# Stream encoder: the sample's transposes and its last key chunk on 128 rows instead of 64

## The chip, the cores and the metric

The kernel runs on one core of one Trainium2 chip. The metric is device time in microseconds (us) of one execution.

## The reference

One inference step of a streaming encoder with four layers, A, B, C, A. Each layer computes x <- x + W_out(mixer(RMSNorm(x)) * silu(gate)) in fp32, and one input projection gives the mixer's inputs and the gate. There are two streams: a prompt of 512 frames without history, and a sample of 64 frames that follows a cache of past keys and values. All widths are for d_model 1024.

```
A: 8 heads of 128; 64-frame chunks attend a band of 9 chunks; bias by clipped distance; RMSNorm on q and k
B: 16 query heads, 4 key heads of 64; window 128 + own chunk; ALiBi, sinks; RMSNorm on q and k
C: latent attention, 16 heads of 64 + 32 rotary; latent of 256; causal by chunk; RMSNorm on q and k
sample: k = concat(cache, own 64 keys): 256 + 64 keys in A and C, 128 + 64 in B
        p = softmax(q k^T * scale + bias);  o = p v
```

Outputs are y for both streams and the new cache rows.

## The kernel before

The 576 frames (TOK) are worked on in five token tiles (TT): four of 128 frames for the prompt and one of 64 (DEC) for the sample. Frames lie on partitions (rows of TensorE's array) wherever a norm is taken, and on columns wherever a projection reads them, so each result is transposed on TensorE by `tr` (L166) into a PSUM tile `t` and copied from there. `tr(out, in_, rows, perm)` loads the data as the stationary operand with as many rows as the tile has frames, and streams that many columns of a permutation: the identity, or a reversed order (flip for 128 frames, flip2 for two halves of 64). For the sample tile rows is 64. These transposes occur in `norm` (two sets of four in each of four layers), in the q and k units of the A layers (four each, in eight head-pair units), in B's key unit (four) and four query units (two each), and in C's query latent (four), key latent (two and one of 32 columns), four query units (four of 96 columns) and eight key and value units (one each).

The large projections are split into a high and a low part in a reduced-width fp32 format (fp32r) and take three products (L151 to L153, L211 to L213); for the sample tile two products do, because its high and low parts lie side by side and fill 128 frames (L156, L157). Scores and value products of softmax are plain fp32 and appear as two TensorE instructions each.

The softmax of the sample has 128 rows: in A and C two heads of 64 queries. Its weights `ex` have 320 columns in A and C: two chunks of 128 cached keys and a last one of 64 own keys; in B there are 128 and 64 for each of two head pairs. They are transposed chunk by chunk; the last chunk is transposed from 64 columns, and its product with the values (`vt[:64, 4]`, L403, L633, L884) uses 64 rows:

```
for c, cn in ((0, 128), (1, 128), (2, 64)):
    tr(pt[:cn, c, :], ex[:, 128 * c : 128 * c + cn], 128, flip2)
S.activation(pts[:, 0:2, :], pt[:, 0:2, :], AF.Copy)
S.activation(pts[:64, 2, :], pt[:64, 2, :], AF.Copy)
PE.matmul(po[:, e, :], vt[:64, 4, 128 * e : 128 * e + 128], pts[:64, 2, r], start=False, stop=True)
```

Buffers rotate: `qs` (results ahead of a transpose) has four, `ex` four, `pts` and the PSUM tile `t` two, the A layers' values `v` two. Within a layer `mix` interleaves the attention of one head pair with the projections of the next pair and the gate of the one before. The order on each engine is then set by the framework's scheduler, which places instructions by simulated times; each engine works through its queue in that order. SyncE issues the DMAs. Layer pools reuse memory as soon as the tile that lay there is done. GpSimd takes the powers for the norms (L104), half of the weight splits (L109), rotary products (L696 to L700), the gate's product (L219) and a few memsets (L353, L821, L822). Layer B's constants, the sinks among them (`sks`, negated at L453 by VectorE), are loaded early.

Of the kernel before, what the change touches and what calls it, by code (L numbers as in the profile page):

```python
# [21 lines left out]
DEC = 64  # L22
# [18 lines left out]
def encoder_step(ctx: ExitStack, tc: tile.TileContext, I, O):  # L41
# [42 lines left out]

    x = []
# [79 lines left out]
    def tr(out, in_, rows, perm=None):  # L165
        PE.transpose(out, in_, (perm or ident)[:rows, :rows])  # L166
# [5 lines left out]
    def norm(t, g, xT):  # L172
        t0, tn = TT[t]
        ss = sb(1, "nss", pool=tiny)[:tn]
        junk = sb(D, "sq", 2, dt=BF16)[:tn]
        S.activation(junk, x[t][:tn], AF.Square, accum_out=ss)
        r = rstd(ss, tn, 1, 1.0 / D)
        for hf in range(2):
            xs = sb(512, "qs", QSB)[:tn]
            cs = slice(hf * 512, hf * 512 + 512)  # L180
            V.scalar_tensor_tensor(out=xs, in0=x[t][:tn, cs], scalar=r, in1=g[:tn, cs], op0=ALU.mult, op1=ALU.mult)
            pt = v3(ps_t(), 128)
            for j in range(4):
                tr(pt[:, j, :tn], xs[:, j * 128 : j * 128 + 128], tn)
            k0 = hf * 4
            l0 = lo_at(t0, TOK)
            hl_evac(xT[:, k0 : k0 + 4, t0 : t0 + tn], xT[:, k0 : k0 + 4, l0 : l0 + tn], pt[:, :, :tn])
            if tn == DEC:
                V.tensor_copy(xT[:, k0 : k0 + 4, 2 * TOK : WT], xT[:, k0 : k0 + 4, TOK : TOK + DEC].bitcast(F32))
# [69 lines left out]
    def layer_a(li, xT, first=None):  # L259
        w = I["a_w_in"][li]  # L260
        with tc.tile_pool(name=f"la{li}", bufs=1, reuse_waits="tile") as lp:
# [7 lines left out]
            def v_units(pr, pieces=None):  # L269
                st = [pieces] if pieces else []  # L270

                def unit(ts, tn):
                    if not st:
                        st.append(load_packed(w, 2048 + 256 * pr, 256))
                    if pr not in vs:
                        vs[pr] = v3(sb(5 * 256, "v", 2, pool=lp), 256)
                    vt = vs[pr]
                    p = ps_mm()
                    for i, t in enumerate(ts):
                        r_ = mm_tok(xT, TOK, 128 * t, tn, st[0], 256, p, 256 * i)  # L280
                    n = len(ts)
                    p = (p if n == 2 else r_)[:, : 256 * n]
                    S.activation(vt[:tn, ts[0] : ts[0] + n, :], v3(p, 256), AF.Copy)
                    for t in ts:
                        ld(O["av"][li, 128 * t : 128 * t + tn, 256 * pr : 256 * pr + 256], vt[:tn, t, :])

                return [lambda ts=ts, tn=tn: unit(ts, tn) for ts, tn in (((0, 1), 128), ((2, 3), 128), ((4,), 64))]

            def qk_units(pr):
                st = []  # L290

                def unit(t, t0, tn):
# [11 lines left out]
                    qs = sb(512, "qs", QSB)[:tn]  # L304
                    V.tensor_tensor(out=v3(qs, 128), in0=v3(p, 128), in1=bc(r.unsqueeze(2), tn, 4, 128), op=ALU.mult)
                    pt = v3(ps_t(), 128)
                    for j in range(4):
                        perm = ident if j > 1 else flip if tn == 128 else flip2
                        tr(pt[:, j, :tn], qs[:, j * 128 : j * 128 + 128], tn, perm)
# [23 lines left out]
            def attn_units(pr):  # L333
# [3 lines left out]
                def soft(s, bias, n):  # L337
                    nm = sb(1, "nm", pool=tiny)
                    tot = sb(1, "tot", pool=tiny)
                    ex = sb(512, "ex", 4)[:, :n]  # L340
                    V.tensor_tensor_reduce(out=ex, in0=s, in1=bias, scale=-1.0, scalar=1e38,
                                           op0=ALU.add, op1=ALU.min, accum_out=nm)
                    S.activation(ex, ex, AF.Exp, bias=nm, scale=-1.0, accum_out=tot)
                    softmax_tail(ex, tot, 128)
                    return ex

                def head(e, t):
# [18 lines left out]
                    for c in range(t + 1):  # L366
                        tr(pt[:, 128 * c : 128 * c + 128], ex[:, 128 * c : 128 * c + 128], 128, flip)
# [8 lines left out]
                def sample():  # L376
# [14 lines left out]
                    ex = soft(s, bs, 320)  # L391
                    pt = v3(ps_t(), 128)
                    for c, cn in ((0, 128), (1, 128), (2, 64)):
                        tr(pt[:cn, c, :], ex[:, 128 * c : 128 * c + cn], 128, flip2)
                    pts = v3(sb(512, "pts", 2), 128)
                    S.activation(pts[:, 0:2, :], pt[:, 0:2, :], AF.Copy)
                    S.activation(pts[:64, 2, :], pt[:64, 2, :], AF.Copy)
                    po = v3(ps_o()[:, :128], 64)
                    for e in range(2):
                        r = slice(64 * e, 64 * e + 64)  # L400
                        for c in range(2):
                            PE.matmul(po[:, e, :], vc[:, c, 128 * e : 128 * e + 128], pts[:, c, r], start=(c == 0), stop=False)
                        PE.matmul(po[:, e, :], vt[:64, 4, 128 * e : 128 * e + 128], pts[:64, 2, r], start=False, stop=True)  # L403
# [31 lines left out]
    def layer_b(xT):  # L435
        w = I["b_w_in"][0]
        with tc.tile_pool(name="lb", bufs=1, reuse_waits="tile") as lp:
# [23 lines left out]
            vt = v3(sb(5 * 256, "v", pool=lp), 256)  # L461
            vc = sb(256, "vc", pool=lp)
# [12 lines left out]
            for t, (t0, tn) in enumerate(TT):  # L475
# [7 lines left out]
                qs = sb(512, "qs", QSB)[:tn]  # L483
                for d in range(2):
                    V.tensor_tensor(out=v4(qs, 2, 64)[:, :, d, :], in0=v3(p[:, :256], 64), in1=bc(r.unsqueeze(2), tn, 4, 64), op=ALU.mult)
                pt = v3(ps_t(), 128)
                for j in range(4):
                    tr(pt[:, j, :tn], qs[:, j * 128 : j * 128 + 128], tn)
# [14 lines left out]
            def q_units(g):  # L503
                w_ = []

                def unit(t, t0, tn):
# [10 lines left out]
                    qs = sb(512, "qs", QSB)[:tn, :256]  # L517
                    V.tensor_tensor(out=v3(qs, 64), in0=v3(p, 64), in1=bc(r.unsqueeze(2), tn, 4, 64), op=ALU.mult)
                    pt = v3(ps_t()[:, :256], 128)
                    for j in range(2):  # L520
                        tr(pt[:, j, :tn], qs[:, j * 128 : j * 128 + 128], tn)
# [19 lines left out]
            def attn_units(g):  # L541
                st = {}

                def head(t):
# [36 lines left out]
                    for c in range(nk // 128):  # L581
                        pt = v4(ps_t(), 2, 128)
                        for e in range(2):
                            for j in range(2):
                                tr(pt[:, e, j, :], exs[e][:, j, 128 * c : 128 * c + 128], 128)
                        pts = v4(sb(512, "pts", 2), 2, 128)
                        if c == 0:
                            S.activation(pts, pt, AF.Copy)
                        else:
                            V.tensor_copy(pts, pt)  # L590
                        ptl.append(pts)
# [8 lines left out]
                def sample():  # L600
# [6 lines left out]
                    ex = v3(sb(512, "ex", 4)[:, :384], 192)  # L607
# [13 lines left out]
                    for j in range(2):  # L621
                        tr(pt[:, 0, j, :], ex[:, j, 0:128], 128)
                        tr(pt[:64, 1, j, :], ex[:, j, 128:192], 128)
                    pts = v4(sb(512, "pts", 2), 2, 128)
                    for c, rows in ((0, 128), (1, 64)):
                        S.activation(pts[:rows, c], pt[:rows, c], AF.Copy)
# [4 lines left out]
                    for e in range(2):  # L631
                        r = slice(64 * e, 64 * e + 64)
                        PE.matmul(po[r], vt[:64, 4, 64 * g : 64 * g + 64], pts[:64, 1, :, r], start=False, stop=True)  # L633
# [7 lines left out]

            run(q_units(0))
# [11 lines left out]
    def layer_c(xT):  # L654
        w = I["c_w_in"][0]
        with tc.tile_pool(name="lc", bufs=1, reuse_waits="tile") as lp:
# [50 lines left out]
            vslot = [v3(sb(7 * 128, f"v{j}", pool=lp), 128) for j in range(2)]  # L707

            pieces = load_chunk(w, [(0, 512)])
            for t, (t0, tn) in enumerate(TT):  # L710
# [5 lines left out]
                c = sb(512, "qs", QSB)[:tn]  # L716
                V.scalar_tensor_tensor(out=c, in0=p, scalar=r, in1=qag[:tn], op0=ALU.mult, op1=ALU.mult)
                pt = v3(ps_t(), 128)
                for j in range(4):
                    tr(pt[:, j, :tn], c[:, j * 128 : j * 128 + 128], tn)  # L720
# [4 lines left out]
            for t, (t0, tn) in enumerate(TT):  # L725
# [6 lines left out]
                c = sb(512, "qs", QSB)[:tn, :256]  # L732
# [4 lines left out]
                kr = sb(32, "kr", 2)[:tn]  # L737
# [4 lines left out]
                for j in range(2):  # L742
                    tr(pt[:, j, :tn], c[:, j * 128 : j * 128 + 128], tn)
                tr(pt[:32, 2, :tn], kr, tn)
# [14 lines left out]
            def q_units(g):  # L759
                st = {}  # L760

                def unit(t, t0, tn):
# [5 lines left out]
                    raw = sb(512, "qs", QSB)[:tn, :384]  # L768
# [12 lines left out]
                    for j in range(4):  # L781
                        tr(pt[:96, j, :tn], qs[:, j, :], tn)
# [6 lines left out]
            def kv_units(pr):  # L789
                kT, vt = kslot[pr % 2], vslot[pr % 2]  # L790

                def unit(ts, tn):
# [9 lines left out]
                    raw = sb(512, "qs", QSB)[:tn, : 128 * n]  # L802
# [9 lines left out]
                    pt = ps_t()[:, : n * tn]  # L812
                    for i in range(n):
                        tr(pt[:, 128 * i : 128 * i + tn], qs[:, 128 * i : 128 * i + 128], tn)
# [9 lines left out]
            def soft(s, n, mask):  # L824
                nm = sb(1, "nm", pool=tiny)
                ex = sb(512, "ex", 4)[:, :n]
# [13 lines left out]
            def attn_units(blk):  # L840
# [4 lines left out]
                def head(t, e):  # L845
# [9 lines left out]
                    for c in range(t + 1):  # L855
                        tr(pt[:, 128 * c : 128 * c + 128], ex[:, 128 * c : 128 * c + 128], 128)
# [11 lines left out]
                def sample():  # L868
# [4 lines left out]
                    ex = soft(s, 320, False)  # L873
                    pt = v3(ps_t(), 128)
                    for c, cn in ((0, 128), (1, 128), (2, 64)):
                        tr(pt[:cn, c, :], ex[:, 128 * c : 128 * c + cn], 128)
                    pts = v3(sb(512, "pts", 2), 128)
                    S.activation(pts[:, 0:2, :], pt[:, 0:2, :], AF.Copy)
                    S.activation(pts[:64, 2, :], pt[:64, 2, :], AF.Copy)
                    po = ps_o()[:, :64]  # L880
                    for c, cn in ((0, 128), (1, 128), (2, 64)):
                        for e in range(2):
                            r = slice(64 * e, 64 * e + 64)
                            PE.matmul(po[r], vt[:cn, 4 + c, r], pts[:cn, c, r], start=(c == 0), stop=(c == 2))  # L884
# [176 lines left out]
```

## Time and profile before

| | |
|---|---|
| median of three runs | 1302.87 us (1301.19 to 1304.98) |
| span of the profiled execution, first to last instruction | 1303.0 us |
| time of the profiled execution beside its span | not recorded apart from the span, which lies between the runs |
| TensorE busy | 1268.8 us (97%), 8119 matmuls or transposes and as many weight loads |
| VectorE, ScalarE, GpSimd busy | 718.3, 651.7, 376.2 us |
| mean granted clock of TensorE | 0.994 of 2.4 GHz |

The busy time of an engine is the time in which it had an instruction in work; matmuls overlap, so TensorE's busy share tells that it had work, not how fast the work went. In the profile's tables PE is TensorE's matmuls and transposes, PEld its weight loads, DVE VectorE, ACT ScalarE, POOL GpSimd; L166 is line 166. A form such as 64*128 64x64 is weights of 64 rows by 128 columns, and 64 rows by 64 columns streamed.

### The profile page before, as it was taken

The page shows a single profiled execution, that of the slowest core. Times are in us where ns is not written, and L with a number is a line of the kernel's source. Part 1 is how long each engine was busy: PE and PEld are TensorE (multiplying, and loading weights), DVE is VectorE, ACT ScalarE, POOL GpSimd, SP SyncE. Part 2 cuts the span into 40 slices and gives each one's busy share as a digit, 9 for nine tenths or more (in the row PEclk, how much of TensorE's full clock was granted, in tenths as well). Part 3 has the DMA queues.
Part 4 walks back from the last instruction along what each step waited for, and adds up shares of the span by engine and source line. Part 5 has one row for each costly group of instructions (what it writes and reads, how often), then busy time and mean ns, then how long its engine had stood idle before and what let it go on. Part 6 is the DMA issues. An engine that isn't in the chain of part 4 may idle for free.

```text
span 1303.0 us, 22559 instructions
## 1 busy us (share of the span) xinstructions
PE 1268.8 (97%) x8119; PEld 1099.4 (84%) x8119; DVE 718.3 (55%) x1983; ACT 651.7 (50%) x1665; POOL 376.2 (29%) x475
## 2 busy tenths in 40 slices
PE   4999999999999999999999999999999999999998
PEld 3889898998889888878898888877788898989986
DVE  3365444452668878626576766676164555444432
ACT  4245353552446766634356767686243454435431
POOL 3231212115025442140275453540401212121150
PEclk9899999999999999999999999999999999999999
DMA  5424141433446312144231101111244251414322
GB/s 160 129 91 137 58 134 51 153 100 95 151 123 215 88 56 80 56 143 147 61 109 45 46 25 50 34 36 49 88 160 128 92 155 54 142 50 134 126 82 73
DMA packets 101727, 127.21 MB, mean 98 GB/s; under 512 B 13296, under 2 KB 79760, under 8 KB 101552
## 3 DMA queue, kind: packets, MB, share of 16 engines
q1 hardware_dynamic: 101616, 125.77, 31.3%
q8 instruction: 64, 1.05, 0.3%
q14 instruction: 47, 0.39, 0.1%
HBM read 105.81 MB, written 24.26 MB: 100 GB/s over the span
## 4 chain that ended last, share of the span: by engine, by line
PE 93%; DMA 3%; DVE 1%; POOL 1%; ACT 1%; issue 1%; SPq 0%; DVEq 0%; ACTq 0%; POOLq 0%
PE mm L151 15%; PE mm L153 15%; PE mm L152 15%; PE t L166 9%; PE mm L211 5%; PE mm L212 5%; PE mm L213 5%; PE mm L156 4%; PE mm L157 4%; PE s L852 3%; PE o L371 3%; PE o L863 2%; PE s L363 2%; PE o L594 1%; DMA sks<-in_b_sinks 1%; DMA x<-in_x 1%
## 5 line engine op out<-in xcount | busy, mean ns | idle before, releaser
L104 POOL TENSOR_TENSOR nv<-nv,mhalf 128x4 f32<-128x4 f32 (+7 forms) x147 | 150.3, 1023 | 489.3 <-DVE nv L103 459.1
L151 PE MATMUL mm<-wh,T 128*128 128x256 f32 (+2 forms) x736 | 246.7, 339 | 3.2 <-ACT T L169 3.2
L153 PE MATMUL mm<-wh,T 128*128 128x256 f32 (+2 forms) x736 | 247.1, 338 | 0.0
L152 PE MATMUL mm<-wl,T 128*128 128x256 f32 (+2 forms) x736 | 244.7, 336 | 0.0
L108 ACT ACTIVATE wh<-ws 128x512 fp32r<-128x512 f32 (+2 forms) x288 | 169.6, 616 | 125.7 <-PE mm L156 74.5
L109 DVE TENSOR_TENSOR wl<-ws,wh 128x512 fp32r<-128x512 f32 (+2 forms) x252 | 170.0, 696 | 47.0 <-ACT wh L108 41.9
L211 PE MATMUL mm<-T,wh 128*128 128x288 f32 x512 | 154.8, 302 | 0.3 <-ACT sq L771 0.3
L213 PE MATMUL mm<-T,wl 128*128 128x288 f32 x512 | 154.1, 301 | 0.0
L151 PEld LDWEIGHTS mm<-wh,T 128*128 128x128 f32 x736 | 141.3, 192 | 15.2 <-ACT T L169 3.8
L212 PE MATMUL mm<-T,wh 128*128 128x288 f32 x512 | 152.8, 298 | 0.0
L153 PEld LDWEIGHTS mm<-wh,T 128*128 128x128 f32 x736 | 141.7, 193 | 12.9 <-issue 0.4
L152 PEld LDWEIGHTS mm<-wl,T 128*128 128x128 f32 x736 | 141.0, 192 | 11.9
L219 POOL TENSOR_TENSOR o<-o,sq 128x288 f32<-128x288 f32 x52 | 44.3, 852 | 227.2 <-DVE sq L217 139.9
L151 PE MATMUL mm<-wh,oT 128*128 128x512 f32 x256 | 99.2, 396 | 2.5 <-ACT oT L238 1.9
L153 PE MATMUL mm<-wh,oT 128*128 128x512 f32 x256 | 99.7, 397 | 1.2 <-POOL oT L241 1.2
L152 PE MATMUL mm<-wl,oT 128*128 128x512 f32 x256 | 100.2, 395 | 0.0
L211 PEld LDWEIGHTS mm<-T,wh 128*128 128x128 f32 x512 | 96.2, 188 | 4.7 <-issue 3.4
L166 PE MATMUL t<-ident,qs 128*128 128x128 f32 (+3 forms) x466 | 78.7, 277 | 20.1 <-DVE T L170 9.1
L212 PEld LDWEIGHTS mm<-T,wh 128*128 128x128 f32 x512 | 96.2, 188 | 1.8 <-issue 1.4
L213 PEld LDWEIGHTS mm<-T,wl 128*128 128x128 f32 x512 | 96.2, 188 | 1.4 <-issue 1.2
L166 PEld LDWEIGHTS t<-ident,qs 128*128 128x128 f32 (+3 forms) x466 | 54.4, 142 | 37.5 <-issue 10.6
L250 DVE TENSOR_TENSOR x<-mm,x 128x512 f32<-128x512 f32 x32 | 21.6, 690 | 112.5 <-PE mm L153 112.4
(233 smaller groups left out, 2666.9 us busy)
## 6 DMA issues: line engine op xcount, KB each, us to landing
ws<-in_a_w_in SPq DMA_DIRECT2D x64, 256.0 KB, 2.9
ws<-in_a_w_in SPq DMA_DIRECT2D x128, 128.0 KB, 2.4
ws<-in_b_w_in SPq DMA_DIRECT2D x40, 256.0 KB, 3.0
ws<-in_a_w_out SPq DMA_DIRECT2D x32, 256.0 KB, 3.2
xd<-x SPq DMA_DIRECT2D x12, 512.0 KB, 2.6
x<-xd SPq DMA_DIRECT2D x12, 512.0 KB, 5.9
ws<-in_c_w_in SPq DMA_DIRECT2D x24, 256.0 KB, 3.3
out_akT<-kf SPq DMA_DIRECT2D x8, 576.0 KB, 3.9
```

The source lines that it names most:

```text
L104: G.tensor_tensor(out=r, in0=r, in1=bc(mhalf[:tn], tn, n), op=ALU.pow)
L108: S.activation(h, src, AF.Copy)
L109: (eng or G).tensor_tensor(out=l, in0=src, in1=h.bitcast(F32), op=ALU.subtract)
L151: PE.matmul(out, xh, h[:, ws], start=(i == 0), stop=False)
L152: PE.matmul(out, xh, l[:, ws], start=False, stop=False)
L153: PE.matmul(out, xl, h[:, ws], start=False, stop=(i == last))
L156: PE.matmul(out, xs, h[:, ws], start=(i == 0), stop=False)
L157: PE.matmul(out, xs, l[:, ws], start=False, stop=(i == last))
L166: PE.transpose(out, in_, (perm or ident)[:rows, :rows])
L211: PE.matmul(p, wh, xT[:, k, cs], start=(k == 0), stop=False)
L212: PE.matmul(p, wh, xT[:, k, ls], start=False, stop=False)
L213: PE.matmul(p, wl, xT[:, k, cs], start=False, stop=(k == KD - 1))
```

## The change

Every transpose uses all 128 rows. The sample's results ahead of a transpose go into one of two standing tiles (`half`), whose lower 64 rows are set to zero once; `tr` no longer takes a row count. The sample's softmax weights go into one standing tile (`exz`) with zeros behind the last key, so that the last chunk is 128 wide; the values' fifth chunk gets zeros in its lower 64 rows by a memset per value tile, and the last product uses 128 rows. The two copies of the transposed weights become one. The framework's DMA scratch is set to 1024 bytes, which makes room. All that is added to the sums is zero.

```diff
+    half = [sb(512, f"half{i}", pool=const) for i in range(2)]
+    exz = sb(512, "exz", pool=const)
+    for z in half:
+        G.memset(z[DEC:], 0.0)
+    G.memset(exz, 0.0)
+    turn = [0]
+
+    def rows_of(tn):
+        if tn == 128:
+            return sb(512, "qs", QSB)
+        turn[0] ^= 1
+        return half[turn[0]]
...
-    def tr(out, in_, rows, perm=None):
-        PE.transpose(out, in_, (perm or ident)[:rows, :rows])
+    def tr(out, in_, perm=None):
+        PE.transpose(out, in_, perm or ident)
...
-            xs = sb(512, "qs", QSB)[:tn]
+            xs = rows_of(tn)
...
-                tr(pt[:, j, :tn], xs[:, j * 128 : j * 128 + 128], tn)
+                tr(pt[:, j, :], xs[:, j * 128 : j * 128 + 128])
...
                         vs[pr] = v3(sb(5 * 256, "v", 2, pool=lp), 256)
+                        G.memset(vs[pr][DEC:, 4, :], 0.0)
...
-                    ex = soft(s, bs, 320)
+                    soft(s, bs, 320, exz[:, :320])
                     pt = v3(ps_t(), 128)
-                    for c, cn in ((0, 128), (1, 128), (2, 64)):
-                        tr(pt[:cn, c, :], ex[:, 128 * c : 128 * c + cn], 128, flip2)
+                    for c in range(3):
+                        tr(pt[:, c, :], exz[:, 128 * c : 128 * c + 128], flip2)
                     pts = v3(sb(512, "pts", 2), 128)
-                    S.activation(pts[:, 0:2, :], pt[:, 0:2, :], AF.Copy)
-                    S.activation(pts[:64, 2, :], pt[:64, 2, :], AF.Copy)
+                    S.activation(pts[:, 0:3, :], pt[:, 0:3, :], AF.Copy)
...
-                        PE.matmul(po[:, e, :], vt[:64, 4, 128 * e : 128 * e + 128], pts[:64, 2, r], start=False, stop=True)
+                        PE.matmul(po[:, e, :], vt[:, 4, 128 * e : 128 * e + 128], pts[:, 2, r], start=False, stop=True)
...
+            G.memset(vt[DEC:, 4, :], 0.0)
...
-                        PE.matmul(po[r], vt[:64, 4, 64 * g : 64 * g + 64], pts[:64, 1, :, r], start=False, stop=True)
+                        PE.matmul(po[r], vt[:, 4, 64 * g : 64 * g + 64], pts[:, 1, :, r], start=False, stop=True)
...
+            G.memset(v3(exz, 256)[:, :, 192:], 0.0)
...
+            for v_ in vslot:
+                G.memset(v_[DEC:, 6, :], 0.0)
+            krz = sb(32, "krz", pool=lp)
+            G.memset(krz[DEC:], 0.0)
+            G.memset(exz[:, 320:384], 0.0)
...
-                            PE.matmul(po[r], vt[:cn, 4 + c, r], pts[:cn, c, r], start=(c == 0), stop=(c == 2))
+                            PE.matmul(po[r], vt[:, 4 + c, r], pts[:, c, r], start=(c == 0), stop=(c == 2))
...
-    nc = _bacc.Bacc("TRN2", target_bir_lowering=False, num_devices=1)
+    nc = _bacc.Bacc("TRN2", target_bir_lowering=False, num_devices=1, dynamic_dma_scratch_size=1024)
```

The other units are edited in the same way as `norm`: `rows_of(tn)` in place of a `qs` tile, and 128 columns written by each transpose, of which the copies still read the first 64.

## Rows read from the trace of the kernel before

**Rows 1.** The page: busy us, share of the span and instructions of each engine.
```profile
PE 1268.8 (97%) x8119; PEld 1099.4 (84%) x8119; DVE 718.3 (55%) x1983; ACT 651.7 (50%) x1665; POOL 376.2 (29%) x475
```

**Rows 2.** Busy us (instructions) of each engine from 700 to 920 us, then granted clock, DMA share, GB/s.
```profile
700.00:920.00 220.00, 217.77 (x1556) 172.15 (x1556) 145.90 (x513) 152.30 (x443) 89.68 (x123) 1.00 0.15 44
```

**Rows 3.** Timeline of TensorE near 390 us: start, us, engine, line, operation, out<-in, form, count.
```profile
389.63 0.28 PE L152 MATMUL mm<-wl,T 128*128 128x256 f32 x1
389.75 0.28 PE L153 MATMUL mm<-wh,T 128*128 128x256 f32 x1
389.87 0.60 PE L166 MATMUL t<-ident,qs 128*128 128x128 f32 x4
...
390.43 0.28 PE L152 MATMUL mm<-wl,T 128*128 128x256 f32 x1
```

**Rows 4.** Timelines of VectorE and of TensorE near 34 us; idle time before and its releaser in brackets.
```profile
34.02 0.17 DVE L453 TENSOR_SCALAR nsks<-sks 128x8 f32<-128x8 f32 x1 [10.23 <-DMA sks<-in_b_sinks]
...
34.84 0.48 PE L166 MATMUL t<-ident,qs 128*128 128x128 f32 x1 [7.74 <-DVE T L170]
```

**Rows 5.** TensorE's groups by form: busy us, mean ns, idle before.
```profile
L166 PE MATMUL t<-ident,qs 64*128 64x64 f32 x74 | 10.5, 237 | 0.8 <-DVE qs L485 0.8
```

**Rows 6.** Timeline of TensorE near 41 us.
```profile
41.11 0.28 PE L152 MATMUL mm<-wl,T 128*128 128x256 f32 x1
41.32 0.46 PE L166 MATMUL t<-ident,qs 64*128 64x64 f32 x4
41.71 0.39 PE L153 MATMUL mm<-wh,T 128*128 128x256 f32 x1
41.93 0.28 PE L151 MATMUL mm<-wh,T 128*128 128x256 f32 x1
```

**Rows 7.** Timeline of TensorE near 131 us.
```profile
130.81 0.38 PE L166 MATMUL t<-flip,ex 128*128 128x128 f32 x2
...
131.03 0.27 PE L166 MATMUL t<-flip,ex 128*64 128x128 f32 x1
131.06 0.48 PE L151 MATMUL mm<-wh,T 128*128 128x512 f32 x1
```

**Rows 8.** Timeline of TensorE near 751 us.
```profile
750.97 0.28 PE L151 MATMUL mm<-wh,lat 128*128 128x256 f32 x1
751.18 0.27 PE L166 MATMUL t<-ident,qs 64*128 64x64 f32 x1
...
751.60 0.29 PE L153 MATMUL mm<-wh,lat 128*128 128x256 f32 x1
```

**Rows 9.** Timeline of TensorE near 268 us.
```profile
267.93 0.29 PE L213 MATMUL mm<-T,wl 128*128 128x288 f32 x1
268.06 0.30 PE L211 MATMUL mm<-T,wh 128*128 128x288 f32 x1
...
268.44 0.29 PE L213 MATMUL mm<-T,wl 128*128 128x288 f32 x1
```

**Rows 10.** Timeline of TensorE near 1078 us, and near 1051 us.
```profile
1077.94 0.55 PE L402 MATMUL o<-pts,vc 128*128 128x64 f32 x4
1078.43 0.43 PE L403 MATMUL o<-pts,v 64*128 64x64 f32 x2
1078.79 0.66 PE L402 MATMUL o<-pts,vc 128*128 128x64 f32 x4
...
1079.74 0.50 PE L151 MATMUL mm<-wh,T 128*128 128x512 f32 x1
...
1050.98 1.05 PE L371 MATMUL o<-pts,v 128*128 128x128 f32 x8
1051.87 0.27 PE L166 MATMUL t<-flip,ex 128*128 128x128 f32 x1
```

**Rows 11.** GpSimd's memsets by form: busy us, mean ns, idle before and its releasers.
```profile
L353 POOL MEMSET bias<- 64x64 f32 x16 | 2.8, 175 | 45.2 <-DMA bias<-in_a_rel 41.1 <-DVE wl L109 4.1
...
L821 POOL MEMSET cmask<- 128x512 f32 x1 | 0.5, 530 | 1.8 <-DVE qs L181 1.8
```

More of the change, by code (lines that the diff above doesn't have):

```diff
@@ L178, in norm @@
         for hf in range(2):
-            xs = sb(512, "qs", QSB)[:tn]
+            xs = rows_of(tn)
             cs = slice(hf * 512, hf * 512 + 512)
-            V.scalar_tensor_tensor(out=xs, in0=x[t][:tn, cs], scalar=r, in1=g[:tn, cs], op0=ALU.mult, op1=ALU.mult)
+            V.scalar_tensor_tensor(out=xs[:tn], in0=x[t][:tn, cs], scalar=r, in1=g[:tn, cs], op0=ALU.mult, op1=ALU.mult)
             pt = v3(ps_t(), 128)
             for j in range(4):
-                tr(pt[:, j, :tn], xs[:, j * 128 : j * 128 + 128], tn)
+                tr(pt[:, j, :], xs[:, j * 128 : j * 128 + 128])
             k0 = hf * 4
@@ L303, in unit @@
                     r = rstd(ss, tn, 4, 1.0 / 128)
-                    qs = sb(512, "qs", QSB)[:tn]
-                    V.tensor_tensor(out=v3(qs, 128), in0=v3(p, 128), in1=bc(r.unsqueeze(2), tn, 4, 128), op=ALU.mult)
+                    qs = rows_of(tn)
+                    V.tensor_tensor(out=v3(qs[:tn], 128), in0=v3(p, 128), in1=bc(r.unsqueeze(2), tn, 4, 128), op=ALU.mult)
                     pt = v3(ps_t(), 128)
@@ L308, in unit @@
                         perm = ident if j > 1 else flip if tn == 128 else flip2
-                        tr(pt[:, j, :tn], qs[:, j * 128 : j * 128 + 128], tn, perm)
+                        tr(pt[:, j, :], qs[:, j * 128 : j * 128 + 128], perm)
                     cs = slice(t0, t0 + tn)
@@ L335, in attn_units, with soft @@
                 st = {}
-                def soft(s, bias, n):
+                def soft(s, bias, n, ex=None):
                     nm = sb(1, "nm", pool=tiny)
                     tot = sb(1, "tot", pool=tiny)
-                    ex = sb(512, "ex", 4)[:, :n]
+                    if ex is None:
+                        ex = sb(512, "ex", 4)[:, :n]
                     V.tensor_tensor_reduce(out=ex, in0=s, in1=bias, scale=-1.0, scalar=1e38,
@@ L366, in head @@
                     for c in range(t + 1):
-                        tr(pt[:, 128 * c : 128 * c + 128], ex[:, 128 * c : 128 * c + 128], 128, flip)
+                        tr(pt[:, 128 * c : 128 * c + 128], ex[:, 128 * c : 128 * c + 128], flip)
                     pts = sb(512, "pts", 2)[:, :nk]
@@ L482, in layer_b @@
                 r = rstd(ss, tn, 4, 1.0 / 64)
-                qs = sb(512, "qs", QSB)[:tn]
+                qs = rows_of(tn)
                 for d in range(2):
-                    V.tensor_tensor(out=v4(qs, 2, 64)[:, :, d, :], in0=v3(p[:, :256], 64), in1=bc(r.unsqueeze(2), tn, 4, 64), op=ALU.mult)
+                    V.tensor_tensor(out=v4(qs[:tn], 2, 64)[:, :, d, :], in0=v3(p[:, :256], 64), in1=bc(r.unsqueeze(2), tn, 4, 64), op=ALU.mult)
                 pt = v3(ps_t(), 128)
                 for j in range(4):
-                    tr(pt[:, j, :tn], qs[:, j * 128 : j * 128 + 128], tn)
+                    tr(pt[:, j, :], qs[:, j * 128 : j * 128 + 128])
                 if t < 4:
@@ L516, in unit @@
                     r = rstd(ss, tn, 4, 1.0 / 64)
-                    qs = sb(512, "qs", QSB)[:tn, :256]
-                    V.tensor_tensor(out=v3(qs, 64), in0=v3(p, 64), in1=bc(r.unsqueeze(2), tn, 4, 64), op=ALU.mult)
+                    qs = rows_of(tn)[:, :256]
+                    V.tensor_tensor(out=v3(qs[:tn], 64), in0=v3(p, 64), in1=bc(r.unsqueeze(2), tn, 4, 64), op=ALU.mult)
                     pt = v3(ps_t()[:, :256], 128)
                     for j in range(2):
-                        tr(pt[:, j, :tn], qs[:, j * 128 : j * 128 + 128], tn)
+                        tr(pt[:, j, :], qs[:, j * 128 : j * 128 + 128])
                     for e in range(2):
@@ L584, in head @@
                             for j in range(2):
-                                tr(pt[:, e, j, :], exs[e][:, j, 128 * c : 128 * c + 128], 128)
+                                tr(pt[:, e, j, :], exs[e][:, j, 128 * c : 128 * c + 128])
                         pts = v4(sb(512, "pts", 2), 2, 128)
@@ L606, in sample @@
                     sums = sb(2, "tot", pool=tiny)
-                    ex = v3(sb(512, "ex", 4)[:, :384], 192)
+                    exf = v3(exz, 256)
+                    ex = exf[:, :, :192]
                     for j in range(2):
@@ L621, in sample @@
                     for j in range(2):
-                        tr(pt[:, 0, j, :], ex[:, j, 0:128], 128)
-                        tr(pt[:64, 1, j, :], ex[:, j, 128:192], 128)
+                        for c in range(2):
+                            tr(pt[:, c, j, :], exf[:, j, 128 * c : 128 * c + 128])
                     pts = v4(sb(512, "pts", 2), 2, 128)
-                    for c, rows in ((0, 128), (1, 64)):
-                        S.activation(pts[:rows, c], pt[:rows, c], AF.Copy)
+                    S.activation(pts, pt, AF.Copy)
                     po = v3(ps_o()[:, :128], 64)
@@ L715, in layer_c @@
                 r = rstd(ss, tn, 1, 1.0 / 512)
-                c = sb(512, "qs", QSB)[:tn]
-                V.scalar_tensor_tensor(out=c, in0=p, scalar=r, in1=qag[:tn], op0=ALU.mult, op1=ALU.mult)
+                c = rows_of(tn)
+                V.scalar_tensor_tensor(out=c[:tn], in0=p, scalar=r, in1=qag[:tn], op0=ALU.mult, op1=ALU.mult)
                 pt = v3(ps_t(), 128)
                 for j in range(4):
-                    tr(pt[:, j, :tn], c[:, j * 128 : j * 128 + 128], tn)
+                    tr(pt[:, j, :], c[:, j * 128 : j * 128 + 128])
                 l0 = lo_at(t0, TOK)
@@ L731, in layer_c @@
                 r = rstd(ss, tn, 2, [(0, 1, 1.0 / 256), (1, 2, 1.0 / 32)])
-                c = sb(512, "qs", QSB)[:tn, :256]
+                cf = rows_of(tn)[:, :256]
+                c = cf[:tn]
                 V.scalar_tensor_tensor(out=c, in0=p[:, :256], scalar=r[:, 0:1], in1=kvg[:tn], op0=ALU.mult, op1=ALU.mult)
@@ L736, in layer_c @@
                 kt = t if t < 4 else 6
-                kr = sb(32, "kr", 2)[:tn]
+                krf = sb(32, "kr", 2) if tn == 128 else krz
+                kr = krf[:tn]
                 rope(kr.unsqueeze(1), y.unsqueeze(1), tabs["c_k_norm"], t, tn, 1)
@@ L742, in layer_c @@
                 for j in range(2):
-                    tr(pt[:, j, :tn], c[:, j * 128 : j * 128 + 128], tn)
-                tr(pt[:32, 2, :tn], kr, tn)
+                    tr(pt[:, j, :], cf[:, j * 128 : j * 128 + 128])
+                tr(pt[:32, 2, :], krf)
                 k0 = 128 * kt
@@ L767, in unit @@
                     p = mm_tok(cq, TOK, t0, tn, pieces, 384)
-                    raw = sb(512, "qs", QSB)[:tn, :384]
+                    rawf = rows_of(tn)[:, :384]
+                    raw = rawf[:tn]
                     S.activation(raw, p, AF.Copy)
@@ L781, in unit @@
                     for j in range(4):
-                        tr(pt[:96, j, :tn], qs[:, j, :], tn)
+                        tr(pt[:96, j, :], v3(rawf, 96)[:, j, :])
                     for j in range(2):
@@ L801, in unit @@
                     p4 = v4(p, 2, 128)
-                    raw = sb(512, "qs", QSB)[:tn, : 128 * n]
+                    rawf = rows_of(tn)[:, : 128 * n]
+                    raw = rawf[:tn]
                     S.activation(v4(raw, 2, 64), p4[:, :, :, :64], AF.Copy)
@@ L811, in unit @@
                     V.tensor_tensor(out=v3(qs, 64), in0=v3(qs, 64), in1=bc(r.unsqueeze(2), tn, 2 * n, 64), op=ALU.mult)
-                    pt = ps_t()[:, : n * tn]
+                    ptf = ps_t()
+                    pt = ptf[:, : n * tn]
                     for i in range(n):
-                        tr(pt[:, 128 * i : 128 * i + tn], qs[:, 128 * i : 128 * i + 128], tn)
+                        tr(ptf[:, 128 * i : 128 * i + 128], rawf[:, 128 * i : 128 * i + 128])
                     k0 = 128 * ts[0]
@@ L825, in soft @@
                 nm = sb(1, "nm", pool=tiny)
-                ex = sb(512, "ex", 4)[:, :n]
+                ex = sb(512, "ex", 4)[:, :n] if mask else exz[:, :n]
                 tot = sb(1, "tot", pool=tiny)
@@ L855, in head @@
                     for c in range(t + 1):
-                        tr(pt[:, 128 * c : 128 * c + 128], ex[:, 128 * c : 128 * c + 128], 128)
+                        tr(pt[:, 128 * c : 128 * c + 128], ex[:, 128 * c : 128 * c + 128])
                     pts = sb(512, "pts", 2)[:, :nk]
@@ L872, in sample @@
                         PE.matmul(s[64 * e : 64 * e + 64], qT[:96, e, SEQ:TOK], kT[:96, e, 512:832], start=True, stop=True)
-                    ex = soft(s, 320, False)
+                    soft(s, 320, False)
                     pt = v3(ps_t(), 128)
-                    for c, cn in ((0, 128), (1, 128), (2, 64)):
-                        tr(pt[:cn, c, :], ex[:, 128 * c : 128 * c + cn], 128)
+                    for c in range(3):
+                        tr(pt[:, c, :], exz[:, 128 * c : 128 * c + 128])
                     pts = v3(sb(512, "pts", 2), 128)
-                    S.activation(pts[:, 0:2, :], pt[:, 0:2, :], AF.Copy)
-                    S.activation(pts[:64, 2, :], pt[:64, 2, :], AF.Copy)
+                    S.activation(pts[:, 0:3, :], pt[:, 0:3, :], AF.Copy)
                     po = ps_o()[:, :64]
-                    for c, cn in ((0, 128), (1, 128), (2, 64)):
+                    for c in range(3):
                         for e in range(2):
                             r = slice(64 * e, 64 * e + 64)
-                            PE.matmul(po[r], vt[:cn, 4 + c, r], pts[:cn, c, r], start=(c == 0), stop=(c == 2))
+                            PE.matmul(po[r], vt[:, 4 + c, r], pts[:, c, r], start=(c == 0), stop=(c == 2))
                     o_evac(tmp[:, SEQ:], po, has)
```

## The prediction

> **What bounds the kernel now.** The page's busy shares come first: TensorE is busy 97% of the span, VectorE, the next, 55% [rows 1]. The busy times by stretch say the same inside a stretch: from 700 to 920 us TensorE works 217.77 of 220 us, at a granted clock of 1.00, which is the 2.4 GHz level, while VectorE and ScalarE work 146 and 152 us [rows 2]. So time is won or lost where TensorE's next instruction starts later than it must. The drawn durations don't tell that, because they overlap: a matmul of 256 columns is drawn 0.28 us long, yet the next one starts 0.12 us after it (389.63 to 389.75 [rows 3]). I therefore read the timeline of TensorE alone and take steps from start to start.
>
> The one long stretch where TensorE is idle is the start: it waits 7.74 us, to 34.84 us, for VectorE, whose queue was held 10.23 us by a copy of layer B's sinks that waits for its DMA [rows 4].
>
> **The change, part by part.** *Transposes with 64 rows.* The program has 107 (74 of the largest form [rows 5], and 16, 16 and 1 of three smaller forms in the same view). On the timeline they stand in 35 groups: 20 of four, 1 of eight, 5 of two, 9 of one.
>
> Four with 64 rows between 256-column matmuls take, from the matmul ahead (41.11) to the second one behind (41.93), 0.82 us [rows 6]. Four with 128 rows in the same setting take 389.75 to 390.43, 0.68 us [rows 3]. The edges are dear: the matmul ahead of the 64-row group has a step of 0.21 instead of 0.12, the one behind it 0.22. The steps within are cheap: (41.71 - 41.32) / 4 = 0.10 us on average, the long last one included, against 0.11 for a 128-row transpose (0.22 for two [rows 7]).
>
> One with 64 rows takes 750.97 to 751.60, 0.63 us [rows 8]. One with 128 rows, between matmuls of 288 columns, takes 268.06 to 268.44, 0.38 us [rows 9]; these matmuls step by 0.13 where those of 256 step by 0.12, so 0.36 at 256 columns. The saving is 0.27 for a group of one and 0.14 for a group of four. A line through both is 0.32 - 0.045 n us for n transposes: a fixed price of about 0.32 us for going to 64 rows and back, less 0.045 us for each transpose that now streams 128 columns. It gives 0.23 for two and -0.04 for the group of eight, where widening costs.
>
> The surroundings change this. Eight groups of four in the attention layers A run straight into 128-row transposes of the softmax, where part of the price overlaps; three in layer C have 96 columns and shorter steps: I take 0.10 for these eleven. Of the five pairs three touch a matmul that fills only 64 columns of the array, where TensorE pays an edge already, and so do most of the single ones: 0.13 instead of 0.23, and 0.18 instead of 0.27. Four groups (near 397, 665, 668 and 688 us: one of the pairs, one single, two of four) stand where TensorE waits for VectorE or GpSimd: nothing. Together: 7 x 0.14 + 11 x 0.10 + 0.23 + 3 x 0.13 + 8 x 0.18 - 0.04 = 4.1 us.
>
> *The sample's value product in the A layers* (L402, L403; eight times). Its rows go 128, 64, 128, 64: 1077.94 to 1079.74, 1.80 us for twelve instructions [rows 10], and the matmul behind pays an edge of some 0.10 as in rows 6. With 128 rows throughout these are twelve plain fp32 instructions; eight such take 1050.98 to 1051.87, 0.89 or 0.111 each [rows 10], so twelve take 1.33. Gain 0.47 + 0.10 = 0.57 each, 4.6 us.
>
> *The same in B (four) and C (eight).* Here the array has 64 columns before and after; only the edge from 128 to 64 rows inside the product goes. The trace has no such product without it. Bounds: the bare entry edge, 0.09 (0.21 - 0.12 [rows 6]), and 0.2, somewhat over half of the 0.32 for both ways. I take the middle, 0.14: 12 x 0.14 = 1.7 us.
>
> *The last key chunk's transposes,* 64 columns wide, become 128 wide. Two with 128 columns start at 130.81, the one with 64 at 131.03, the matmul behind at 131.06 [rows 7]: 0.11 per transpose and no edge, so nothing is won or lost. The Trainium skill (TensorEngine Tiling (Array Packing), Key Properties) says "Changing tiling mode (not just tile) drains the TensorE", and lists 128x64 as a mode. By that rule these 24 transposes would pay edges too, and more would be won (rival 4); rows 6 and 8 bear it out for 64 rows, rows 7 don't for transposes of 64 columns.
>
> *The rest.* ScalarE loses one of two copies in each of 20 samples: not the bound, zero. GpSimd gets 17 memsets. Rows 11 have 0.175 us for 64x64 and 0.53 for 128x512, which no new one exceeds: 3 to 9 us, spread over the whole program. The first three come while GpSimd waits for the first input; those at the head of a layer wait until the memory under them is free. Cost: zero, as long as no power or weight split behind them in GpSimd's queue is what TensorE waits for next; up to 9 us if each showed in full. The two standing buffers for 64-row results and the one for the sample's exponentials replace rotating ones; they are reused a head pair later, or after the other buffer, so I see no wait, cost zero; with one, a sample would stand like the groups near 397 us. They also free slots of the four-slot rotation. The smaller DMA scratch makes room, zero.
>
> **Sum.** 4.1 + 4.6 + 1.7 = 10.4 us. The profiled execution spans 1303.0 us, 0.1 above the median of the runs and between their ends: 1303.0 - 10.4 = 1292.6, and against the median 1292.5 us (-0.8%).
>
> **Rivals.**
> 1. *The savings are partly waited away*, or the scheduler, which orders each engine by simulated times, orders the units less well. If nothing of layer C's part (some 2.8 us) arrives and 2 us more go at the edges of layers: 1297.3. For: four 64-row groups stand beside stalls already. Against: 2.2 us idle in 220 in layer C [rows 2].
> 2. *The start moves.* The sinks' copy stands in VectorE's queue where the scheduler's simulation had a hole; the new buffers let the sample's norm go earlier and may fill that hole. If all of the 7.74 us goes: 1284.8. Against: the same DMA times are simulated as before.
> 3. *Rows don't matter, only streamed columns.* Then the edges come from something else, and stay. Widening costs 107 x 0.045 = 4.8 us and the products gain nothing: 1307.8. It decides if the edges of 128-row groups are no cheaper. Against: rows 10, where all stream 64 columns, only the rows differ, and two 64-row instructions take 0.36 us (1078.43 to 1078.79) where two of 128 rows take 0.22. The Trainium skill (TensorE: Matmul & The Clock Gate, Why this matters for your kernels) says that a matmul with K=32 takes the time of one with K=128, which speaks for this rival. By that page's gaps for 64 and 128 columns an estimate is 0.03 us for each widened transpose and 1306 for the whole; rows 10 agree only away from the edges.
> 4. *64-column transposes pay edges too:* 24 round trips of 0.3 us go as well, 1285.3. Against: rows 7.
> 5. *A memset holds GpSimd's queue.* In the A layers each head pair clears a strip of its value buffer; if it waits for that buffer's readers, the powers of the norms stand behind it and TensorE runs out of work. It ends slower from 14.3 us of idle on (10.4 and 0.3%), 1.8 us in each of eight pairs; at the 41.1 us that the memsets of today wait in total [rows 11], 1333.6. Against: those waits cost TensorE nothing, and the last readers of a value buffer are two pairs back.
>
> **How the numbers follow.** A measurement of this kernel tells about 0.3% (3.9 us) from no change. Forecast, 1289 to 1296: 0.60. Rival 1: 0.18, of which 0.07 within 0.3%. Rival 2: 0.11. Rival 3: 0.04, half of it within 0.3%. Rival 4: 0.02. Rival 5: 0.05, of which 0.02 slower by more. Faster 0.60 + 0.11 + 0.11 + 0.02 = 0.84, same 0.07 + 0.02 + 0.03 = 0.12, slower 0.04. The range reaches from most of rival 2 (1285.5) to a little past rival 1 (1298).
>
> **What would show it.** Right: among TensorE's groups by form no transpose with 64 rows is left; four transposes of the sample take 0.68 to 0.70 where they took 0.82; A's product takes 1.33 us instead of 1.80; the other engines' busy times hardly move. Wrong: steps of 0.2 at the same edges with 128 rows (rival 3); a VectorE or GpSimd wait ahead of TensorE that is new, or an idle start that changed by over 2 us (rivals 2 and 5); more changes to 64-column matmuls because units interleave otherwise (rival 1).

## The result, and the profile after

The changed kernel takes 1293.0 us (median of four runs, 1291.81 to 1294.44) where the kernel before takes 1302.65: a ratio of 0.9917 (95% interval 0.9897 to 0.9937). The forecast was 1292.5.

The page of the changed kernel has TensorE 11.9 us less busy and the other engines within 5 us of where they were [rows 1]:

```profile
PE 1256.9 (97%) x8119; PEld 1098.1 (85%) x8119; DVE 714.1 (55%) x1983; ACT 650.2 (50%) x1645; POOL 380.0 (29%) x492
```

As many matmuls and transposes, 20 ScalarE instructions fewer, 17 GpSimd instructions more. TensorE stays at 97% of a shorter span, so its busy share says nothing of where the gain arose; its timeline does. First the places that answer to rows 6 and 8, a group of four and a group of one between 256-column matmuls, both now on 128 rows:

```profile
38.65 0.28 PE L164 MATMUL mm<-wh,T 128*128 128x256 f32 x1
38.77 0.28 PE L165 MATMUL mm<-wl,T 128*128 128x256 f32 x1
38.88 0.60 PE L179 MATMUL t<-ident,half 128*128 128x128 f32 x4
39.24 0.36 PE L166 MATMUL mm<-wh,T 128*128 128x256 f32 x1
39.44 0.28 PE L164 MATMUL mm<-wh,T 128*128 128x256 f32 x1
...
741.21 0.28 PE L165 MATMUL mm<-wl,lat 128*128 128x256 f32 x1
741.33 0.27 PE L179 MATMUL t<-ident,half 128*128 128x128 f32 x1
741.35 0.37 PE L166 MATMUL mm<-wh,lat 128*128 128x256 f32 x1
741.55 0.28 PE L164 MATMUL mm<-wh,lat 128*128 128x256 f32 x1
```

The matmul ahead of the group has its plain step again, 0.12 (38.65 to 38.77, and 38.77 to 38.88), where it was 0.21. The group of four takes 38.77 to 39.44, 0.67 us instead of 0.82; the group of one 741.21 to 741.55, 0.34 instead of 0.63.

Next the sample's value product in an A layer [rows 10], one in B and one in C, on the same kernel's timeline:

```profile
132.93 0.55 PE L416 MATMUL o<-pts,vc 128*128 128x64 f32 x4
133.32 0.39 PE L417 MATMUL o<-pts,v 128*128 128x64 f32 x2
...
134.18 0.48 PE L164 MATMUL mm<-wh,T 128*128 128x512 f32 x1
134.50 0.39 PE L165 MATMUL mm<-wl,T 128*128 128x512 f32 x1
...
445.76 0.44 PE L645 MATMUL o<-pts,vc 128*64 128x128 f32 x4
446.03 0.39 PE L648 MATMUL o<-pts,v 128*64 128x128 f32 x4
446.35 0.44 PE L179 MATMUL t<-ident,half 128*128 128x128 f32 x2
...
755.27 0.34 PE L165 MATMUL mm<-wl,lat 128*128 128x384 f32 x1
755.44 0.34 PE L166 MATMUL mm<-wh,lat 128*128 128x384 f32 x1
755.71 0.57 PE L909 MATMUL o<-pts,v 128*64 128x64 f32 x12
756.21 0.33 PE L179 MATMUL t<-ident,ex 128*128 128x128 f32 x1
```

And the kernel before in the same products of B and C:

```profile
448.64 0.44 PE L630 MATMUL o<-pts,vc 128*64 128x128 f32 x4
449.01 0.43 PE L633 MATMUL o<-pts,v 64*64 64x128 f32 x4
449.38 0.33 PE L166 MATMUL t<-ident,qs 64*128 64x64 f32 x2
...
765.94 0.71 PE L884 MATMUL o<-pts,v 128*64 128x64 f32 x12
766.58 0.33 PE L166 MATMUL t<-ident,ex 128*128 128x128 f32 x1
```

A's twelve instructions took 1.80 and take 1.25 us (132.93 to 134.18), B's eight 0.74 and 0.59, C's twelve 0.64 and 0.50. The products not shown agree: all eight of A take 1.79 to 1.80 before and 1.25 to 1.26 now. (B's and C's last ones contain a wait in both kernels, and are shorter by the same 0.15 and 0.14.)

The start has hardly moved. VectorE's copy of the sinks waits 10.39 us (10.23 in rows 4), and TensorE with it 8.19 (7.74):

```profile
32.94 0.17 DVE L467 TENSOR_SCALAR nsks<-sks 128x8 f32<-128x8 f32 x1 [10.39 <-DMA ws<-in_a_w_in]
...
33.76 1.12 PE L179 MATMUL t<-ident,qs 128*128 128x128 f32 x4 [8.19 <-DVE T L183]
```

The releaser is named another DMA here; which of the DMAs under way it was is inferred from the time at which each one ended.

### The profile page after: what moved, and what is told of

Read it like the earlier page. It is cut to its first block, busy times and chain, and to the rows that moved or that the text cites. A ratio compares the mean times of both kernels' runs of the same rounds, so it can differ in the third digit from the quotient of the medians.

```text
span 1289.7 us, 22565 instructions
## 1 busy us (share of the span) xinstructions
PE 1256.9 (97%) x8119; PEld 1098.1 (85%) x8119; DVE 714.1 (55%) x1983; ACT 650.2 (50%) x1645; POOL 380.0 (29%) x492
## 4 chain that ended last, share of the span: by engine, by line
PE 93%; DMA 2%; ACT 2%; DVE 1%; POOL 1%; SPq 1%; issue 1%; ACTq 0%; DVEq 0%; POOLq 0%
PE mm L164 15%; PE mm L166 15%; PE mm L165 15%; PE t L179 9%; PE mm L224 5%; PE mm L226 5%; PE mm L225 5%; PE mm L169 4%; PE mm L170 4%; PE o L386 3%; PE s L878 3%; PE o L889 2%; PE s L378 2%; PE o L609 1%; PE s L578 1%
## 5 line engine op out<-in xcount | busy, mean ns | idle before, releaser
L179 PE MATMUL t<-ident,qs 128*128 128x128 f32 (+1 forms) x376 | 65.4, 283 | 18.7 <-DVE T L183 9.3
L179 PEld LDWEIGHTS t<-ident,qs 128*128 128x128 f32 (+1 forms) x376 | 45.9, 142 | 30.5 <-DVE T L183 8.5
```

Of the source, the lines that this page charges most:

```text
L179: PE.transpose(out, in_, perm or ident)
```

## The experiments

The theory: TensorE pays a fixed price each time it goes between instructions on 128 and on 64 rows; the change removes these passages and pays for it with wider transposes. The rivals: only streamed columns count; the price is per 64-row instruction; the gain is a better order of the units, or the start; GpSimd's memsets cost something. Each kernel was timed beside the kernel before on the same chip; ratios are to that.

**The transposes alone.** The last key chunk goes back to 64 rows; the standing tile and the memsets stay.

```diff
-                    for c in range(3):
-                        tr(pt[:, c, :], exz[:, 128 * c : 128 * c + 128], flip2)
+                    for c, cn in ((0, 128), (1, 128), (2, 64)):
+                        tr(pt[:cn, c, :], exz[:, 128 * c : 128 * c + cn], flip2)
...
-                        PE.matmul(po[:, e, :], vt[:, 4, 128 * e : 128 * e + 128], pts[:, 2, r], start=False, stop=True)
+                        PE.matmul(po[:, e, :], vt[:64, 4, 128 * e : 128 * e + 128], pts[:64, 2, r], start=False, stop=True)
```

> The last key chunk is transposed from 64 columns and multiplied on 64 rows again, as in the kernel before; the sample's other transposes keep 128 rows. Theory (a fixed price for each change of TensorE between 64 and 128 rows): 1302.65 - 4.1 = 1298.5 us, range 1296.5 to 1300.5; the product in the A layers takes 1.80 us again. Rival (only streamed columns count): 107 transposes cost 0.045 us more each, 1307.5 us. Rival (the changed kernel is faster because the units happen to be ordered better): no step of the trace differs, and the time is anywhere between 1293 and 1303.

Measured: 1299.32 us, ratio 0.9968 (0.9955 to 0.9980), which is 4.2 us of 1302.65 saved. The theory's 4.1 fits, though the interval only bounds the saving to between 2.6 and 5.9 us; the columns rival, which had the kernel slower, falls. The product in the A layers takes 1.80 us again in this kernel's timeline (134.42 to 136.22), so steps differ, and where the theory has them: a better order of the units alone would have left them as they were.

**The product alone.** The reverse: `tr` takes the tile's row count again, the chunk stays wide.

```diff
-    def tr(out, in_, perm=None):
-        PE.transpose(out, in_, perm or ident)
+    def tr(out, in_, perm=None, tn=128):
+        rows, cols = (128, 128) if tn == 128 else (64, 64)
+        PE.transpose(out[:, :cols], in_[:rows], (perm or ident)[:rows, :cols])
...
-                tr(pt[:, j, :], xs[:, j * 128 : j * 128 + 128])
+                tr(pt[:, j, :], xs[:, j * 128 : j * 128 + 128], None, tn)
```

The other calls for the sample's results are edited in the same way.

> The sample's transposes go back to 64 rows and 64 columns; the last key chunk keeps 128 rows. In the product the streamed columns are the same 64 in both kernels, only rows differ. Theory (a fixed price per change of rows): 1302.65 - 4.6 - 1.7 = 1296.4 us, range 1294.5 to 1298.5. Rival (only streamed columns count): 1302.6 us.

Measured: 1296.23 us, ratio 0.9947 (0.9935 to 0.9959), 6.9 us saved where 6.3 was expected. As many columns are streamed in these products as before, so columns can't be what was saved. The two halves add up: 4.2 + 6.9 = 11.1 us, against 10.8 by the ratio of the whole change.

**Half of the transposes wide, in alternation.** The sharpest test of "per passage": in each group every second transpose is on 64 rows. There are 49 transposes on 64 rows and 49 passages there and back (the count of 51 in the expectation was a slip).

```diff
+    def tr(out, in_, perm=None, tn=128, j=1):
+        rows, cols = (128, 128) if tn == 128 or j % 2 else (64, 64)
+        PE.transpose(out[:, :cols], in_[:rows], (perm or ident)[:rows, :cols])
...
-                tr(pt[:, j, :], xs[:, j * 128 : j * 128 + 128])
+                tr(pt[:, j, :], xs[:, j * 128 : j * 128 + 128], None, tn, j)
```

> As the changed kernel, but in each group of the sample's transposes the first and the third of four (the first of two) have 64 rows again, the others 128. 49 transposes of the 107 are on 64 rows, with 51 changes to 64 rows and back where the kernel before has 35 groups. Theory (a price per change, not per transpose): each group of four makes two round trips, 0.45 us more than with 128 rows; 18 x 0.45 + 0.9 for the group of eight + 0.8 for the pairs = 9.8 us over the changed kernel, 1302.8 us, range 1300.5 to 1305: as slow as the kernel before or slower, though over half of its transposes are wide. Rival (a price per 64-row transpose): 49 of 107 of the transposes' 4.1 us come back, 1294.9 us. Rival (only streamed columns count): 49 narrow ones save 0.045 each, 1290.8 us.

Measured: 1303.88 us, ratio 0.9997 (0.9986 to 1.0008). All that the change gains is gone again, product included, although over half of the transposes are wide and fewer 64-row instructions are left than before. A price per 64-row transpose (1294.9) and one for columns (1290.8) both lie below every run of this kernel (1301.59 to 1305.25). A group of four in this kernel's timeline, of which two are on 64 rows (the row shows the form of the first):

```profile
370.03 0.39 PE L164 MATMUL mm<-wh,T 128*128 128x512 f32 x1
370.35 0.99 PE L180 MATMUL t<-ident,half 64*128 64x64 f32 x4
371.10 0.48 PE L165 MATMUL mm<-wl,T 128*128 128x512 f32 x1
```

From the first transpose to the matmul behind it is 0.75 us (370.35 to 371.10), with 128 rows 0.36 (38.88 to 39.24 above), and with 64 rows throughout 0.39 (41.32 to 41.71 [rows 6]). Mixing the two kinds costs twice as much as either alone.

**Every added memset twice.**

```diff
     G.memset(exz, 0.0)
+    G.memset(exz, 0.0)
...
                         G.memset(vs[pr][DEC:, 4, :], 0.0)
+                        G.memset(vs[pr][DEC:, 4, :], 0.0)
```

> Every memset that the change adds stands twice, one behind the other. In the changed kernel's trace the 17 take 5.2 us of GpSimd. Theory (they are hidden): 1293.0 us, range 1291.5 to 1294.5, with the same steps on TensorE. Rival (a memset holds GpSimd's queue): up to 5.2 us more, 1298.2 us.

Measured: 1292.89 us, ratio 0.9923 (0.9910 to 0.9935): no difference from the changed kernel. GpSimd's busy time in its profile is 386.0 us, in the changed kernel's 380.0; 6 us more of GpSimd cost nothing. This shows that the memsets' own time is hidden. It doesn't test the other half of rival 5, a memset that holds the queue while it waits, since the second of a pair has nothing left to wait for. That is read from the changed kernel's trace. Its longest such wait is 14.0 us (the group's line: line, engine, operation, form, count, then busy us, mean ns, idle before and releaser):

```profile
L728 POOL MEMSET exz<- 128x64 f32 x1 | 0.2, 156 | 14.0 <-PE t L179 14.0
```

TensorE doesn't stand behind it: its waits for GpSimd add up to 1.7 us in this trace and to 2.8 in that of the kernel before.

**The changed kernel again.**

> The changed kernel once more, beside a run of the kernel before on the same chip, as the measure for the next one. Theory (10.4 us saved): 0.992 of the kernel before. Rival (the first four runs caught a good state of the start): above 0.995.

Measured: 1292.74 us, ratio 0.9906 (0.9883 to 0.9928). The gain is there again, beside other runs of the kernel before.

**The start.** Rival 2 priced the wait at the start, which the change left alone. It can be taken away: the table that is late holds elements of one that VectorE already has.

```diff
-                ld(sks[64 * e : 64 * e + 64], I["b_sinks"].rearrange("o (j e) -> o j e", e=2)[:, :, e].to_broadcast([64, 8]))
+                V.tensor_copy(sks[64 * e : 64 * e + 64], sk[64 * e : 64 * e + 64].rearrange("p (j e) -> p e j", e=2)[:, e])
```

> The changed kernel, with one edit more: the small table of layer B's sinks (sks) is copied by VectorE from the one that is loaded anyway (sk), in place of two DMAs of single elements. In the changed kernel's trace VectorE is still held 10.39 us at 32.94 us, and TensorE idles from 25.4 to 33.8 us. Theory (that idle time is the wait for this DMA alone): about 8 us less than the changed kernel, 1285 us or 0.986 of the kernel before, range 1283 to 1288. Rival (the weights that are loaded at the same time, or another constant's DMA, are as late): the wait shows a new releaser and less than 3 us are gained, 1290 to 1293 us.

Measured: 1285.16 us, ratio 0.9853 (0.9831 to 0.9874); 7.6 us less than the changed kernel beside the same runs of the kernel before, and the fastest kernel measured here. Its timeline of VectorE and then of TensorE at the start:

```profile
22.60 0.17 DVE L462 TENSOR_SCALAR nsk<-sk 128x16 f32<-128x16 f32 x1 [1.93 <-DMA sk<-in_b_sinks]
22.68 0.34 DVE L465 COPY sks<-sk 64x8 f32<-64x8 f32 x2
23.05 1.29 DVE L183 TENSOR_TENSOR T<-t,T 128x512 fp32r<-128x512 f32 x2
24.26 0.16 DVE L467 TENSOR_SCALAR nsks<-sks 128x8 f32<-128x8 f32 x1
...
23.89 1.03 PE L179 MATMUL t<-ident,qs 128*128 128x128 f32 x4 [2.09 <-DVE T L183]
```

The hold of 10.39 us is gone, the small wait for `sk` (1.93 us) stays, and TensorE idles 2.09 us before its transposes where it idled 8.19. In the kernel before, the chain of work that ended last goes over the table's DMA, 12.04 us long, up to the copy at 34.02 us [rows 4]:

```profile
21.89 12.04 DMA sks<-in_b_sinks
```

The idle time is 6.1 us shorter, the gain 7.6. The granted clock may give the rest: around the wait TensorE worked 5.3 us at 0.50, the 1.2 GHz level, in the changed kernel's profile (23.07 to 25.40 and 33.76 to 36.73 us) and 3.5 us at 0.51 in this one (23.89 to 27.40). Half of that difference, some 0.9 us, is an estimate of what it gives back. No run tried that apart.

## Why the prediction was right

*Groups of transposes.* The line 0.32 - 0.045 n holds at all sizes that the trace has undisturbed: 0.15 for four (0.14 forecast), 0.29 for one (0.27), 0.23 for two (0.23; 414.62 to 415.31 before, 408.28 to 408.74 now). For the group of eight it gave a loss of 0.04, and a loss came, 0.05, from 1.07 us in the kernel before to 1.12 in the changed one:

```profile
985.00 0.28 PE L152 MATMUL mm<-wl,T 128*128 128x256 f32 x1
985.21 0.71 PE L166 MATMUL t<-ident,qs 64*128 64x64 f32 x8
...
986.07 0.28 PE L151 MATMUL mm<-wh,T 128*128 128x256 f32 x1
...
974.25 0.28 PE L165 MATMUL mm<-wl,T 128*128 128x256 f32 x1
974.37 1.04 PE L179 MATMUL t<-ident,half 128*128 128x128 f32 x8
...
975.37 0.28 PE L164 MATMUL mm<-wh,T 128*128 128x256 f32 x1
```

Groups that run into softmax's transposes gained the 0.10 that was taken (171.57 to 172.25 before, 168.17 to 168.75 now). The total, 4.1, measured alone as 4.2; that they agree to 0.1 is partly luck. The four groups that were said to stand beside waits were taken at nothing. The pair and the four near 665 and 688 us are 0.65 and 0.70 us shorter in the changed kernel's profile (664.60 to 665.78 before, 657.53 to 658.06 now; 686.96 to 688.35, 682.19 to 682.88), where no wait stands beside them any more. The single one near 668 stood beside none and gained 0.25 (667.76 to 668.38, 659.77 to 660.14). The four near 397 are 0.13 longer (395.94 to 398.14, 390.41 to 392.74).

*A's product.* The size was right, 0.57 each. Before, from rows 10 to the start of the second matmul behind, 1077.94 to 1080.08, it was 2.14 us; now it is 1.57 (132.93 to 134.50):

```profile
1080.08 0.39 PE L152 MATMUL mm<-wl,T 128*128 128x512 f32 x1
```

Its split was not right: 0.55 fell inside the product, where 0.47 was forecast, and only 0.02 on the matmul behind it, where 0.10 was. The run of twelve takes 1.25 us, less than the 1.33 of twelve times 0.111, and the matmul behind it has a step of 0.32 (134.18 to 134.50) where it had 0.34.

*B's and C's.* 0.15 and 0.14 measured for the 0.14 that was taken between 0.09 and 0.2. The bounds were read, the middle was not; that it hit so closely is luck.

*The last chunk's 64-column transposes* paid no edge, so rival 4 had nothing to win: in the trace of before 20 of the 24 start 0.11 us behind the transpose ahead, as wide ones do (the other four, second behind a value product into 64 columns, at 0.16 to 0.17, as wide ones there do in the changed kernel). The Trainium skill lists 128x64 among its modes (TensorEngine Tiling (Array Packing), Tiling Modes), from which rival 4 took that they would pay; these steps don't bear that reading out. The value products into 64 columns do pay: in the rows of C above the 384-column matmul has a step of 0.17 (755.27 to 755.44), and the one ahead of the product 0.27.

*The rest.* The memsets cost nothing, as doubling them showed. The copies and the standing buffers were not tried apart; the changed kernel's trace has no wait of VectorE or ScalarE for a reader of the standing tiles, and the sum comes out without them. Of rival 1 the other order came, in layer C, but not the loss. Rivals 2 and 5 didn't come about, rival 3 is excluded by the two halves and by the alternation. Its sentence in the Trainium skill, that few rows cost what 128 cost (TensorE: Matmul & The Clock Gate, Why this matters for your kernels), leaves out the passage between them, and that is what these runs measure.

*The base of the sum.* One step was loose. The profiled execution of before was taken to lie 0.1 us from the median. The runs of the changed kernel list span and time together (1289.7 and 1291.81), and the time is 2.1 us above the span; so that execution was one of about 1305, the slowest of its three, and by its own time the sum is 1294.6. The number given stood against the median, 1292.5. The two profiles differ by 13.3 us, more than the runs: before A's first value product (135.77 and 132.93 on the two timelines) 2.8 us are between them, where some 0.5 of the forecast lies. From there to the last matmul (1297.21 and 1283.87), at a granted clock of 1.00 in both, it is 10.5, where 9.9 was forecast: 1.9 up to the first A layer's last value product (294.46 and 289.76; 1.9 forecast), 6.2 from there over layers B and C to the second A layer's first (1077.94 and 1067.03; 5.5 forecast) and 2.4 behind it (2.5 forecast). So the A layers came out as added up, and B and C as a sum: there the units interleave otherwise than before (C's third product stands behind a 384-column matmul at 797.90 before, behind a transpose at 786.95 now), and what each single transpose gained isn't known. The rest belongs to the start, whose length differs between executions: in the profiles of the other kernels that keep the wait that product starts at 133.8 to 135.7. Here the wait ends 1.08 us earlier (34.84 and 33.76), and behind it TensorE works at a granted clock of 0.50, the 1.2 GHz level, for 5.7 us in the kernel before (to 40.56) and for 3.0 in the changed one (to 36.73), which by half of the difference is an estimated 1.4 us more.

## What to carry to other kernels

On a kernel that TensorE bounds, look for instructions on fewer rows between full ones, and price the passage, not the instruction: here a round trip costs about 0.32 us, as much as three full transposes, so padding with zeros to 128 rows pays up to about seven transposes in a row by the line, and with eight it lost 0.05. Read such prices as steps from start to start on the timeline, and test them by alternation: if mixing two kinds is dearer than either, the passage is what costs. When a large wait stays where it was (the start here), it is worth its own experiment; it held 7.6 us, where the whole change gave some 10.

## What the runs showed of the hardware

- A round trip from 128 to 64 rows on TensorE costs some 0.32 us at a granted clock of 1.00, apart from what runs inside. Weight loads show where: on the changed kernel's timeline of weight loads the transposes' first load starts about 0.1 us before the transpose (38.79, 38.88), on that of before with it (41.31, 41.32). That the load can't be brought forward over the passage is a reading of these rows; no run tried it apart.

```profile
38.65 0.19 PEld L165 LDWEIGHTS mm<-wl,T 128*128 128x128 f32 x1
38.79 0.46 PEld L179 LDWEIGHTS t<-ident,half 128*128 128x128 f32 x4
```

```profile
40.99 0.19 PEld L152 LDWEIGHTS mm<-wl,T 128*128 128x128 f32 x1
41.31 0.33 PEld L166 LDWEIGHTS t<-ident,qs 64*128 64x128 f32 x4
```

- Transposes whose weights have 64 columns pay no passage here (steps of 0.11 us), value products into 64 columns do (0.10 us at the entry in the rows of C).
- Two DMAs of single elements, 128 x 8 numbers in all, held VectorE for 10.4 us (12.04 for the DMA in the chain of the kernel before); two copies of 0.17 us each did the same work.
